# Feed-forward of a decoder trunk: the weight sums of the next column pair are traced amid a pair, the second product starts with another of its seven quarter products, and the residual tiles are loaded back one at a time

## The chip, the cores and the metric

One Trainium2 chip, of which the kernel uses one core (core 0). The time is device microseconds of one whole execution. Before the change three runs took 1507.84, 1508.0 and 1511.98 us; the median is 1508.0 us. The profiled execution took 1507.54 us, of which 1505.8 us are the span that the trace covers.

## The reference

The kernel computes one decoder layer on 1024 rows of width 1024 in float32: three groups of attention heads, an output projection, and a feed-forward part. All that the change touches is the feed-forward part and the final norm:

```python
h2 = rmsnorm(x, norm2_g[l])
u = jnp.square(jax.nn.relu(jnp.einsum('bsd,df->bsf', h2, w_1[l])))   # 1024 -> 4096
x = x + jnp.einsum('bsf,fd->bsd', u, w_2[l])                         # 4096 -> 1024
...
return rmsnorm(x, final_g)
```

## The kernel before

**Precision.** Every float32 factor is split into a high and a low part (hi by ScalarE, lo = value - hi by VectorE), and a product is three matmuls: hi x hi, hi x lo, lo x hi. TensorE is "PE" in the rows, its unit of work here is a matmul of 128x128 weights by 512 columns.

**First product.** The 4096 columns of W1 are worked in 16 pairs of 2 x 128. The first four pairs (NP0) are plain (`hidden`). Pairs 4 to 15 go through `pair_products`: a pair's product is a 2x2 matrix of quarters, and seven quarter products in place of eight are taken, each 12 matmuls (L1339 to L1341), in this order of weights: b11, t2, t3, t1, b21, t4, b22. Here b11, b21, b22 are quarters of the weights themselves; t1 to t4 are sums of quarters, worked out on the chip. On the other side stand quarters of the rows or their sums s1 to s4 (tiles `sr` in the rows), made beforehand.

`pair_weights` makes a pair's weights: two loads of 512 KB (tiles `raw`, L1312, issued by SyncE, "SP"), the split of the first tile (w1h on ScalarE L1327, w1l on VectorE L1328), the four sums (tiles `tr`, VectorE L1324), and their splits (tiles `tw`: hi on ScalarE L1318, lo on VectorE L1319). It is called at the head of `pair_products`, so in the text of the program a pair's weight work stands behind all work of the pair before.

After each quarter product `into` adds it into a half of a hidden tile `ut` (VectorE, L1355), `squared` applies ReLU and square (ScalarE, L1344 and L1345), and at a pair's end five combinations of the four halves (tiles `us`, VectorE L1390) and two halves themselves are written to DRAM, as `u_d[i, j]`; those seven writes are issued by ScalarE (L1391 to L1393).

**Second product.** Seven quarter products again, each over all 16 pairs: `operands(i, spec, j)` loads `u_d[i, j]` (tile `uw`, L1243) and either one quarter of W2 into the same tile (L1246) or two quarters into a tile `w2q` (L1249, L1250), which VectorE adds or subtracts (L1251). Then ScalarE writes the high part (`uwh`, L1254) and VectorE the low (`uwl`, L1255), and 12 matmuls follow (L1399 to L1401). In the table `products` five of seven need two quarters; those at index i = 2 and i = 1 need one. The first four operand sets are requested during the last pair (`ahead`). When a quarter product is finished, it is added into the residual tiles `xa` (L1462), which were stored in DRAM (`xa_d`) and come back by eight loads of 512 KB (L1455), all issued behind the step (n, j) = (0, 4), and behind them in the text nothing else of that step.

**What sets the order.** Each engine runs its instructions in one fixed order. A scheduler (the tile framework) sets it when the kernel is built, from the order of the Python text, the dependences and its own costs; an instruction whose input or buffer is not ready holds up all that stand behind it on that engine. Buffers are pools: `ut`, `tw`, `uw`, `w2q` and `sraw` share ten 4 KB buffers; `raw` has two; `tr` and `us` share eight; `w1h` and `w1l` share four. All PSUM tiles (names pt, psd, s, po in the rows) share eight banks.

Of the kernel before, what the change touches and what calls it, by code (L numbers as in the profile page):

```python
# [19 lines left out]
DM = 1024  # L20
DFF = 4096
NB = 8
# [52 lines left out]
def dap(ap, offset, dims):  # L75
    return bass.AP(tensor=ap.tensor, offset=ap.offset + offset, ap=dims)
# [3 lines left out]
def trunk_kernel(ctx, tc, x, norm1_g, w_in, b_f, lam_q1, lam_k1, lam_q2, lam_k2,  # L80
# [3 lines left out]
    dma = nc.sync.dma_start  # L84
# [28 lines left out]
    def utile(shape, dt, name):  # L113
        return up.tile(shape, dt, tag="u", name=name)
# [7 lines left out]
    def wtile(shape, dt, name):  # L122
        return wp.tile(shape, dt, tag="w", name=name)
# [7 lines left out]
    def ttile(shape, name):  # L131
        return tp.tile(shape, F32, tag="t", name=name)
# [5 lines left out]
    state = {}  # L138
# [40 lines left out]
    def bcast_row(vec, n, name):  # L179
        t = ttile([P, n], name)  # L180
        dma(t, dap(vec, 0, [[0, P], [1, n]]))
        return t
# [1013 lines left out]
    def bank():  # L1196

        p, tag, name = banks[turn[0] % len(banks)]
        turn[0] += 1
        return p.tile([P, 512], F32, tag=tag, name=name)  # L1200
# [3 lines left out]
    NP = DFF // (2 * P)  # L1204
    u_d = dp.tile([7, NP, P, 512], F32, name="u_d")

    def hidden(ws, ut, half):
        (wh, wl), cs = ws, slice(half * 512, (half + 1) * 512)
        ps = bank()
        for k in range(8):  # L1210
            hh = h2[0][half][k // 2][:, k % 2, :]
            hl = h2[1][half][k // 2][:, k % 2, :]
            T.matmul(ps, wh[:, k, :], hh, start=(k == 0), stop=False)
            T.matmul(ps, wh[:, k, :], hl, start=False, stop=False)
            T.matmul(ps, wl[:, k, :], hh, start=False, stop=(k == 7))
        A.activation(ut[:, cs], ps, AF.Relu)
        V.scalar_tensor_tensor(ut[:, cs], ps, 0.0, ut[:, cs], op0=ALU.max, op1=ALU.mult)
# [3 lines left out]
    def w2q(j, right, n):  # L1221
        r0 = (2 * j + right) * P
        return w_2[r0:r0 + P, n * 512:(n + 1) * 512]

    add, sub = ALU.add, ALU.subtract
    products = (
        (0, ((0, 0), (1, 1), add), ((0, 0, add), (1, 1, add))),
        (5, ((0, 1), (1, 1), sub), ((0, 1, add), (1, 1, add))),
        (2, ((1, 1), None, None), ((0, 0, sub), (0, 1, add))),
        (6, ((1, 0), (0, 0), sub), ((0, 0, add), (1, 0, add))),  # L1230
        (4, ((1, 0), (1, 1), add), ((0, 0, add),)),
        (1, ((0, 0), None, None), ((1, 0, add), (1, 1, sub))),
# [5 lines left out]
    def operands(i, spec, j):  # L1238

        alloc = ptile if made[0] % 10 < 2 else htile  # L1240
        made[0] += 1
        raw = utile([P, 2, 512], F32, "uw")
        dma(raw[:, 0, :], u_d[i, j])  # L1243
        q0, q1, op = spec
        if q1 is None:
            dma(raw[:, 1, :], w2q(j, *q0))  # L1246
        else:
            two = utile([P, 2, 512], F32, "w2q")
            dma(two[:, 0, :], w2q(j, *q0))  # L1249
            dma(two[:, 1, :], w2q(j, *q1))  # L1250
            V.tensor_tensor(raw[:, 1, :], two[:, 0, :], two[:, 1, :], op=op)  # L1251
        hi = alloc([P, 2, 512], F32R, "uwh")
        lo = alloc([P, 2, 512], F32R, "uwl")
        A.activation(hi, raw, AF.Copy)  # L1254
        V.tensor_tensor(lo, raw, hi.bitcast(F32), op=ALU.subtract)  # L1255
        return hi, lo
# [3 lines left out]
    NP0 = 4  # L1260
# [48 lines left out]
    def pair_weights(j):  # L1309
        r0, r1 = (rp.tile([P, 8, P], F32, tag="r", name="raw") for _ in range(2))  # L1310
        for r, ft in ((r0, 2 * j), (r1, 2 * j + 1)):
            dma(r, w_1[:, ft * P:(ft + 1) * P].rearrange("(k p) n -> p k n", p=P))  # L1312
        h0, l0 = (wtile([P, 8, P], F32R, n) for n in ("w1h", "w1l"))
        q0, q1 = slice(0, 4), slice(4, 8)
        w = dict(b11=(h0[:, q0], l0[:, q0]), b21=(h0[:, q1], l0[:, q1]))

        def split(name, raw, both):
            A.activation(both[:, 0], raw, AF.Copy)  # L1318
            V.tensor_tensor(both[:, 1], raw, f32(both[:, 0]), op=sub)  # L1319
            w[name] = both[:, 0], both[:, 1]  # L1320

        def weight_sum(name, p0, p1):
            raw = qtile([P, 4, P], F32, "tr")
            V.tensor_tensor(raw, p0, p1, op=sub)  # L1324
            split(name, raw, utile([P, 2, 4, P], F32R, "tw"))
            return raw
        A.activation(h0, r0, AF.Copy)  # L1327
        V.tensor_tensor(l0, r0, f32(h0), op=sub)  # L1328
        t1 = weight_sum("t1", r1[:, q0], r0[:, q0])
        t2 = weight_sum("t2", r1[:, q1], t1)  # L1330
        weight_sum("t3", r1[:, q1], r1[:, q0])
        weight_sum("t4", r0[:, q1], t2)
        split("b22", r1[:, q1], tp.tile([P, 2, 4, P], F32R, tag="t", name="b22"))
        return w
# [8 lines left out]
    def squared(a):  # L1343
        A.activation(a, a, AF.Relu)  # L1344
        A.activation(a, a, AF.Square)  # L1345

    def pair_products(j, ut):

        w = pair_weights(j)
        a11, a21, a12, a22 = ut[0][:, :512], ut[0][:, 512:], ut[1][:, :512], ut[1][:, 512:]  # L1350

        def into(dst, src, a, b):
            ps = bank()
            quarter_product(ps, a, w[b])
            V.tensor_tensor(dst, src, ps, op=add)  # L1355
            return ps
        ps = bank()
        quarter_product(ps, a11q, w["b11"])
        A.activation(a11, ps, AF.Copy)
        into(a12, a11, rows_sum["s2"], "t2")  # L1360
        into(a21, a12, rows_sum["s3"], "t3")
        p5 = into(a22, a21, rows_sum["s1"], "t1")
        V.tensor_tensor(a12, a12, p5, op=add)
        squared(a22)
        for dst, a, b in ((a11, a12q, "b21"), (a21, a22q, "t4"), (a12, rows_sum["s4"], "b22")):
            into(dst, dst, a, b)
            squared(dst)

    ahead = []
    for j in range(NP):  # L1370
        if j == NP - 1:
            ahead += [operands(0, products[0][1], t) for t in range(2)]
        ws, ut = [], []
        for ft in (2 * j, 2 * j + 1):
            if j < NP0:
                ws.append(load_split(w_1[:, ft * P:(ft + 1) * P].rearrange("(k p) n -> p k n", p=P),
                                     [P, 8, P], "w1"))
            ut.append(utile([P, S], F32, "ut"))
        if j < NP0:
            for i, half in ((0, 0), (1, 0), (0, 1), (1, 1)) if j < 2 else ((0, 0), (0, 1), (1, 0), (1, 1)):  # L1380
                hidden(ws[i], ut[i], half)
        else:
            pair_products(j, ut)
        a11, a21, a12, a22 = ut[0][:, :512], ut[0][:, 512:], ut[1][:, :512], ut[1][:, 512:]
        for i, p0, p1, op in ((0, a11, a22, add), (3, a21, a11, sub), (1, a21, a22, add),
                              (2, a11, a12, add), (4, a12, a22, sub)):
            if j == NP - 1 and i == 2:
                ahead += [operands(0, products[0][1], len(ahead) + t) for t in range(2)]
            st = qtile([P, 512], F32, "us")
            V.tensor_tensor(st, p0, p1, op=op)  # L1390
            A.dma_start(u_d[i, j], st)  # L1391
        A.dma_start(u_d[5, j], a11)
        A.dma_start(u_d[6, j], a22)  # L1393
        row_sums(j)
# [49 lines left out]
    for n, (i, spec, dsts) in enumerate(products):  # L1444
        ps = [bank() for _ in range(4)]
        stag = STAG if n == len(products) - 1 else 0
        for j in range(NP - stag):
            ops = ahead.pop(0) if ahead else operands(i, spec, j)
            for m in range(4):
                accumulate(ps[m], m, ops, j == 0, j == NP - 1)  # L1450
            if (n, j) == (0, 4):
                gf_bc = bcast_row(final_g, DM, "gf_bc")
                for sb in range(NB):
                    xa[sb] = vtile([P, DM], F32, "xa") if sb < 6 else ttile([P, DM], "xa")
                    dma(xa[sb], xa_d[sb])  # L1455
        kept = [operands(i, spec, j) for j in range(NP - stag, NP)]
        for m in range(4):
            for j, ops in enumerate(kept):
                accumulate(ps[m], m, ops, False, j == stag - 1)
            for r, c, op in dsts:  # L1460
                x_q = xa[4 * r + m][:, c * 512:(c + 1) * 512]
                V.tensor_tensor(x_q, x_q, ps[m], op=op)  # L1462
            if n == 4:
                finish_row(m)
            elif n == 5:
                begun.append(begin_row(4 + m))
            elif stag:
                end_row(4 + m, begun[m])
# [29 lines left out]
```

## Time and profile before

| what | us |
|---|---|
| median of three runs (lowest, highest) | 1508.0 (1507.84, 1511.98) |
| profiled execution | 1507.54 |
| its span | 1505.8 |
| TensorE (PE) busy | 1428.2, 95% |
| VectorE (DVE) busy | 1008.8, 67% |
| ScalarE (ACT) busy | 728.9, 48% |
| GpSimd (POOL) busy | 175.4, 12% |

The span begins at the first instruction of the trace. The attention part and the first four column pairs fill it up to about 927 us; pairs 4 to 15 run up to 1185.3, the second product up to 1497.5, and the last norm and store up to the end. The number behind a tile name in the order listings is a running number of the build, so a tile of the same pair can have two numbers in the two kernels. "PEclk" is the clock that was granted to TensorE as a share of full speed (2.4 GHz); 0.50 is 1.2 GHz. A row of busy times reads: stretch in us, its length, busy us (and number of instructions) of PE, of its weight loads, of DVE, ACT and POOL, then PEclk, the DMA engines' busy share, and GB/s. In a timeline the bracket at a row's end is how long the engine had been idle and what released it.

### The profile page before, as it was taken

Reading aid. Unit: us, or ns where it says so; the run is one execution under the profiler, and the core shown is the slowest. Engines: PE = TensorE matmul, PEld = TensorE weight load, DVE = VectorE, ACT = ScalarE, POOL = GpSimd, SP = SyncE. Lnnn points to the kernel's source line nnn. Section 1 sums busy time; section 2 is a strip of 40 time slices with the busy share of each in tenths; the row PEclk is TensorE's granted clock in tenths of the full one; section 3 lists DMA queues with packets and bytes.
Section 4 is the critical chain, followed back from the end, with each engine's and each line's share of the span. In section 5 each row is a group of like instructions: output and inputs, shape, how many; then the busy total and the mean of one; then the engine's idle time right before and its main releaser. Section 6 shows DMA issues by size and latency. Waiting matters only on the chain.

```text
span 1505.8 us, 21003 instructions
## 1 busy us (share of the span) xinstructions
PE 1428.2 (95%) x7427; PEld 1185.5 (79%) x7427; DVE 1008.8 (67%) x2090; ACT 728.9 (48%) x1421; POOL 175.4 (12%) x125
## 2 busy tenths in 40 slices
PE   7999999999999989988899998999989899999997
PEld 7988877797878889876687786787768688888886
DVE  5535357757685555577977985577767588786783
ACT  5345456656575555447533423345444335343542
POOL 1021111102022212222301120000000000000000
PEclk8999999999999999999999999999999999999999
DMA  6334455444423121388315243344435899888661
GB/s 219 61 105 115 114 161 148 123 117 118 103 65 98 52 64 38 91 187 259 103 36 161 73 145 133 105 148 153 133 126 180 305 336 366 296 298 270 228 230 56
DMA packets 164265, 230.28 MB, mean 153 GB/s; under 512 B 14942, under 2 KB 89182, under 8 KB 164160
## 3 DMA queue, kind: packets, MB, share of 16 engines
q1 hardware_dynamic: 143232, 194.33, 42.7%
q10 hardware_dynamic: 20928, 34.61, 6.2%
q8 instruction: 58, 0.95, 0.3%
q14 instruction: 47, 0.39, 0.1%
HBM read 170.86 MB, written 56.85 MB: 151 GB/s over the span
## 4 chain that ended last, share of the span: by engine, by line
PE 55%; DVE 6%; ACT 4%; DMA 3%; issue 2%; SPq 0%; ACTq 0%; POOL 0%; DVEq 0%; POOLq 0%
PE pt L1399 3%; PE pt L1400 3%; PE pt L1401 3%; PE po L458 2%; PE psd L296 2%; PE psd L298 2%; PE psd L297 2%; PE pt L438 2%; PE s L1399 2%; PE pt L1339 2%; PE s L1400 2%; PE s L1401 2%; PE pt L1341 2%; PE pt L1340 2%; PE psd L1399 1%
## 5 line engine op out<-in xcount | busy, mean ns | idle before, releaser
L1254 ACT ACTIVATE uwh<-uw 128x1024 fp32r<-128x1024 f32 x112 | 116.2, 1057 | 160.5 <-DVE uw L1251 40.1
L1255 DVE TENSOR_TENSOR uwl<-uw,uwh 128x1024 fp32r<-128x1024 f32 x112 | 134.3, 1222 | 48.1 <-ACT uwh L1254 47.8
L296 PE MATMUL psd<-hT,wqh 128*128 128x512 f32 x384 | 159.2, 414 | 0.4 <-DVE kl L412 0.3
L298 PE MATMUL psd<-hT,wql 128*128 128x512 f32 x384 | 154.1, 401 | 0.9 <-POOL wql L282 0.9
L297 PE MATMUL psd<-hT,wqh 128*128 128x512 f32 x384 | 152.7, 398 | 0.0
L442 DVE TENSOR_TENSOR pTl<-pt,pTh 128x512 fp32r<-128x512 f32 (+1 forms) x160 | 99.6, 631 | 56.1 <-ACT pTh L441 54.7
L326 PE MATMUL psd<-wvh,hT 128*128 128x256 f32 (+1 forms) x384 | 115.1, 301 | 2.9 <-ACT hT L204 1.8
L327 PE MATMUL psd<-wvl,hT 128*128 128x256 f32 (+1 forms) x384 | 110.6, 289 | 2.3 <-POOL wvl L282 2.3
L328 PE MATMUL psd<-wvh,hT 128*128 128x256 f32 (+1 forms) x384 | 110.0, 288 | 0.0
L438 PE MATMUL pt<-ident,prow 128*128 128x128 f32 x572 | 94.5, 278 | 10.6 <-ACT prow L503 7.3
L441 ACT ACTIVATE pTh<-pt 128x512 fp32r<-128x512 f32 (+1 forms) x160 | 86.2, 548 | 37.4 <-PE pt L438 34.5
L282 POOL TENSOR_TENSOR wql<-raw,wqh 128x1024 fp32r<-128x1024 f32 x24 | 58.2, 2428 | 291.6 <-ACT wqh L281 291.6
L438 PEld LDWEIGHTS pt<-ident,prow 128*128 128x128 f32 x572 | 68.9, 142 | 27.4 <-ACT prow L503 11.8
L298 PEld LDWEIGHTS psd<-hT,wql 128*128 128x128 f32 x384 | 72.7, 189 | 15.9 <-POOL wql L282 1.9
L296 PEld LDWEIGHTS psd<-hT,wqh 128*128 128x128 f32 x384 | 73.0, 190 | 11.8 <-DVE kl L412 0.6
L297 PEld LDWEIGHTS psd<-hT,wqh 128*128 128x128 f32 x384 | 72.9, 190 | 10.3
L326 PEld LDWEIGHTS psd<-wvh,hT 128*128 128x128 f32 x384 | 74.4, 194 | 6.3 <-ACT hT L204 3.8
L1390 DVE TENSOR_TENSOR us<-ut 128x512 f32<-128x512 f32 x80 | 54.6, 715 | 34.8 <-ACT ut L1345 34.7
L327 PEld LDWEIGHTS psd<-wvl,hT 128*128 128x128 f32 x384 | 74.7, 194 | 3.9 <-POOL wvl L282 2.9
L458 PE MATMUL po<-pTh,vt 128*128 128x128 f32 (+1 forms) x284 | 73.7, 280 | 4.2 <-ACT pTh L441 3.1
L328 PEld LDWEIGHTS psd<-wvh,hT 128*128 128x128 f32 x384 | 74.3, 194 | 1.5 <-issue 0.8
L458 PE MATMUL po<-pTl,vt 128*128 128x128 f32 (+1 forms) x284 | 71.4, 293 | 3.5 <-DVE pTl L442 3.0
(381 smaller groups left out, 3823.6 us busy)
## 6 DMA issues: line engine op xcount, KB each, us to landing
w2q<-in_w_dram SPq DMA_DIRECT2D x160, 256.0 KB
uw<-u_d SPq DMA_DIRECT2D x112, 256.0 KB
u_d<-us ACTq DMA_DIRECT2D x80, 256.0 KB
raw<-in_w_in_dram SPq DMA_DIRECT2D x34, 512.0 KB
raw<-in_w_dram SPq DMA_DIRECT2D x32, 512.0 KB
sa<-aqk_d SPq DMA_DIRECT2D x32, 256.0 KB
u_d<-ut ACTq DMA_DIRECT2D x32, 256.0 KB
uw<-in_w_dram SPq DMA_DIRECT2D x32, 256.0 KB
```

The source lines that it names most:

```text
L296: T.matmul(ps, wh[:, k, :], hh, start=(k == 0), stop=False)
L297: T.matmul(ps, wh[:, k, :], hl, start=False, stop=False)
L298: T.matmul(ps, wl[:, k, :], hh, start=False, stop=(k == 7))
L326: T.matmul(dst, hh, wh[:, k % 4, :], start=(k == 0), stop=False)
L327: T.matmul(dst, hh, wl[:, k % 4, :], start=False, stop=False)
L328: T.matmul(dst, hl, wh[:, k % 4, :], start=False, stop=(k == 7))
L438: T.transpose(pt[:, i * P:(i + 1) * P], b, ident)
L442: V.tensor_tensor(lo[:, :n], pt[:, :n], hi[:, :n].bitcast(F32), op=ALU.subtract)
L458: T.matmul(po[:, cols:cols + n], lhs, pT[part][:, c0:c0 + n], start=(first and part == 0), stop=(last and part == 1))
L1254: A.activation(hi, raw, AF.Copy)
L1255: V.tensor_tensor(lo, raw, hi.bitcast(F32), op=ALU.subtract)
L1399: T.matmul(ps, hi[:, 0, ms], hi[:, 1, :], start=first, stop=False)
```

## The change

Three edits, none of which adds or removes an instruction; on each engine there are as many after as before.

1. `pair_weights(j + 1)` is called in the middle of pair j, behind the fourth quarter product and its `squared`, and for pair 4 behind the last plain pair. The weights are handed over in `state["w"]`.
2. In `products` the rows stand in the order i = 2, 5, 0, 6, 4, 1, 3 in place of 0, 5, 2, 6, 4, 1, 3: the second product begins with one of the two that need a single quarter of W2 (two loads of 256 KB for a step, no sum on VectorE). `ahead` names its index accordingly.
3. The residual tiles are requested one at a time, behind every second step of the first of these seven, each placed in SyncE's order behind the latest `uw` load (`tc.issue_after`); the load of the final norm's gains (L181 in `bcast_row`) moves to (n, j) = (1, 0).

```diff
@@ -1224,9 +1224,9 @@
 
     add, sub = ALU.add, ALU.subtract
     products = (
+        (2, ((1, 1), None, None), ((0, 0, sub), (0, 1, add))),
+        (5, ((0, 1), (1, 1), sub), ((0, 1, add), (1, 1, add))),
         (0, ((0, 0), (1, 1), add), ((0, 0, add), (1, 1, add))),
-        (5, ((0, 1), (1, 1), sub), ((0, 1, add), (1, 1, add))),
-        (2, ((1, 1), None, None), ((0, 0, sub), (0, 1, add))),
         (6, ((1, 0), (0, 0), sub), ((0, 0, add), (1, 0, add))),
         (4, ((1, 0), (1, 1), add), ((0, 0, add),)),
         (1, ((0, 0), None, None), ((1, 0, add), (1, 1, sub))),
@@ -1240,7 +1240,7 @@
         alloc = ptile if made[0] % 10 < 2 else htile
         made[0] += 1
         raw = utile([P, 2, 512], F32, "uw")
-        dma(raw[:, 0, :], u_d[i, j])
+        state["uw"] = dma(raw[:, 0, :], u_d[i, j]).ins
         q0, q1, op = spec
         if q1 is None:
             dma(raw[:, 1, :], w2q(j, *q0))
@@ -1346,7 +1346,7 @@
 
     def pair_products(j, ut):
 
-        w = pair_weights(j)
+        w = state["w"]
         a11, a21, a12, a22 = ut[0][:, :512], ut[0][:, 512:], ut[1][:, :512], ut[1][:, 512:]
 
         def into(dst, src, a, b):
@@ -1362,6 +1362,8 @@
         p5 = into(a22, a21, rows_sum["s1"], "t1")
         V.tensor_tensor(a12, a12, p5, op=add)
         squared(a22)
+        if j + 1 < NP:
+            state["w"] = pair_weights(j + 1)
         for dst, a, b in ((a11, a12q, "b21"), (a21, a22q, "t4"), (a12, rows_sum["s4"], "b22")):
             into(dst, dst, a, b)
             squared(dst)
@@ -1369,7 +1371,7 @@
     ahead = []
     for j in range(NP):
         if j == NP - 1:
-            ahead += [operands(0, products[0][1], t) for t in range(2)]
+            ahead += [operands(products[0][0], products[0][1], t) for t in range(2)]
         ws, ut = [], []
         for ft in (2 * j, 2 * j + 1):
             if j < NP0:
@@ -1379,13 +1381,15 @@
         if j < NP0:
             for i, half in ((0, 0), (1, 0), (0, 1), (1, 1)) if j < 2 else ((0, 0), (0, 1), (1, 0), (1, 1)):
                 hidden(ws[i], ut[i], half)
+            if j == NP0 - 1:
+                state["w"] = pair_weights(NP0)
         else:
             pair_products(j, ut)
         a11, a21, a12, a22 = ut[0][:, :512], ut[0][:, 512:], ut[1][:, :512], ut[1][:, 512:]
         for i, p0, p1, op in ((0, a11, a22, add), (3, a21, a11, sub), (1, a21, a22, add),
                               (2, a11, a12, add), (4, a12, a22, sub)):
             if j == NP - 1 and i == 2:
-                ahead += [operands(0, products[0][1], len(ahead) + t) for t in range(2)]
+                ahead += [operands(products[0][0], products[0][1], len(ahead) + t) for t in range(2)]
             st = qtile([P, 512], F32, "us")
             V.tensor_tensor(st, p0, p1, op=op)
             A.dma_start(u_d[i, j], st)
@@ -1448,11 +1452,13 @@
             ops = ahead.pop(0) if ahead else operands(i, spec, j)
             for m in range(4):
                 accumulate(ps[m], m, ops, j == 0, j == NP - 1)
-            if (n, j) == (0, 4):
-                gf_bc = bcast_row(final_g, DM, "gf_bc")
-                for sb in range(NB):
+            if n == 0 and j % 2 == 0:
+                sb = j // 2
+                with tc.issue_after(state["uw"]):
                     xa[sb] = vtile([P, DM], F32, "xa") if sb < 6 else ttile([P, DM], "xa")
                     dma(xa[sb], xa_d[sb])
+            if (n, j) == (1, 0):
+                gf_bc = bcast_row(final_g, DM, "gf_bc")
         kept = [operands(i, spec, j) for j in range(NP - stag, NP)]
         for m in range(4):
             for j, ops in enumerate(kept):
```

The first listing is VectorE's order before the change, at the end of pair 9 and the start of pair 10. `ut_10571` and `us_...` belong to pair 9; `tr_10737` to `tw_10754` are pair 10's weight sums and their low parts, and `ut_10728<-ut_10727,psd_10774` takes up pair 10's second quarter product (the one with t2).

```order
L1355 TENSOR_TENSOR ut_10571<-ut_10571,s_10694 128x512
L1390 TENSOR_TENSOR us_10716<-ut_10570,ut_10571 128x512
L1390 TENSOR_TENSOR us_10719<-ut_10570,ut_10571 128x512
L1390 TENSOR_TENSOR us_10722<-ut_10571 128x512
L1324 TENSOR_TENSOR tr_10737<-raw_10730,raw_10729 128x512
L1324 TENSOR_TENSOR tr_10742<-raw_10730,tr_10737 128x512
L1324 TENSOR_TENSOR tr_10747<-raw_10730 128x512
L1319 TENSOR_TENSOR tw_10739<-tr_10737,tw_10739 128x512
...
L1319 TENSOR_TENSOR tw_10754<-tr_10752,tw_10754 128x512
L1355 TENSOR_TENSOR ut_10728<-ut_10727,psd_10774 128x512
```

The same place after the change: the `tr` and `tw` tiles that follow pair 9's last `us` are those of pair 11 (10827 and up). Those of pair 10 stand one pair earlier, behind pair 8's last `us`.

```order
L1394 TENSOR_TENSOR us_10750<-ut_10601,ut_10602 128x512
L1394 TENSOR_TENSOR us_10753<-ut_10602 128x512
L1324 TENSOR_TENSOR tr_10827<-raw_10820,raw_10819 128x512
L1324 TENSOR_TENSOR tr_10832<-raw_10820,tr_10827 128x512
L1355 TENSOR_TENSOR ut_10759<-ut_10758,psd_10774 128x512
L1319 TENSOR_TENSOR tw_10829<-tr_10827,tw_10829 128x512
L1319 TENSOR_TENSOR tw_10834<-tr_10832,tw_10834 128x512
L1324 TENSOR_TENSOR tr_10837<-raw_10820 128x512
L1355 TENSOR_TENSOR ut_10758<-ut_10759,s_10788 128x512
L1324 TENSOR_TENSOR tr_10842<-raw_10819,tr_10832 128x512
L1319 TENSOR_TENSOR tw_10839<-tr_10837,tw_10839 128x512
```

So pair 10's sums no longer stand between pair 9's last combination and the quarter product of pair 10 that needs them; the sums found there have a whole pair until they are due.

TensorE's order before at the start of pair 10: `pt_10760` is its first quarter product (with w1h and w1l), `pt_10802` the fourth (tw_10739, which is t1), `pt_10819` the fifth (b21, a half of w1h), and `psd_10774` the second (tw_10744, which is t2).

```order
L1339 MATMUL pt_10760<-h2001_8821,w1h_10733 128x512
L1340 MATMUL pt_10760<-h2101_8825,w1h_10733 128x512
L1341 MATMUL pt_10760<-h2001_8821,w1l_10734 128x512
L1339 MATMUL pt_10802<-sr_9461,tw_10739 128x512
L1340 MATMUL pt_10802<-sr_9463,tw_10739 128x512
L1339 MATMUL pt_10819<-h2002_8822,w1h_10733 128x512
L1339 MATMUL psd_10774<-sr_9630,tw_10744 128x512
L1340 MATMUL psd_10774<-sr_9632,tw_10744 128x512
```

And after the change, the same place:

```order
L1339 MATMUL pt_10760<-h2001_8821,w1h_10666 128x512
L1340 MATMUL pt_10760<-h2101_8825,w1h_10666 128x512
L1341 MATMUL pt_10760<-h2001_8821,w1l_10667 128x512
L1339 MATMUL psd_10774<-sr_9630,tw_10677 128x512
L1340 MATMUL psd_10774<-sr_9632,tw_10677 128x512
L1341 MATMUL psd_10774<-sr_9630,tw_10677 128x512
L1339 MATMUL psd_10774<-sr_9630,tw_10677 128x512
L1340 MATMUL psd_10774<-sr_9632,tw_10677 128x512
```

Before, single matmuls of three quarter products stand mixed behind the first one; after, the twelve of the second product follow the twelve of the first without anything between.

SyncE's order before, at the start of the second product; `xa` are the residual tiles, of which one has been requested earlier and seven stand here in a row ahead of the next operand set (`uw_11801`, the sixth of its product, whose two w2q loads follow).

```order
L1455 DMA xa_11787<-xa_d_8751 128x1024
L1455 DMA xa_11789<-xa_d_8751 128x1024
L1455 DMA xa_11791<-xa_d_8751 128x1024
L1455 DMA xa_11793<-xa_d_8751 128x1024
L1455 DMA xa_11795<-xa_d_8751 128x1024
L1455 DMA xa_11797<-xa_d_8751 128x1024
L1455 DMA xa_11799<-xa_d_8751 128x1024
L1243 DMA uw_11801<-u_d_9168 128x512
```

After, the stretch that begins with the fourth operand set (each now has two loads, both into `uw`):

```order
L1243 DMA uw_11682<-u_d_9168 128x512
L1246 DMA uw_11682<-in_w_2_dram 128x512
L1459 DMA xa_11713<-xa_d_8751 128x1024
L1459 DMA xa_11739<-xa_d_8751 128x1024
L1243 DMA uw_11753<-u_d_9168 128x512
L1246 DMA uw_11753<-in_w_2_dram 128x512
L1459 DMA xa_11772<-xa_d_8751 128x1024
L1243 DMA uw_11774<-u_d_9168 128x512
```

The residual loads now stand singly or in twos between operand sets.

## Rows read from the trace of the kernel before

**Rows 1.** Busy time by stage, in the columns told above.

```profile
927.10:1185.30 258.20, 242.69 (x1013) 191.89 (x1012) 179.52 (x270) 115.33 (x179) 0.00 (x0) 0.97 0.44 150
1185.30:1208.50 23.20, 17.22 (x67) 13.79 (x66) 10.69 (x14) 6.14 (x8) 0.00 (x0) 0.85 1.01 374
1208.50:1497.50 289.00, 288.99 (x1275) 238.91 (x1273) 211.05 (x284) 120.99 (x143) 0.00 (x0) 1.00 0.76 260
```

**Rows 2.** Same view, every stretch with half clock between 927 and 1210.

```profile
935.35:938.76 3.41, 3.20 (x8) 2.53 (x9) 1.36 (x3) 0.59 (x2) 0.00 (x0) 0.50 0.96 284
959.24:962.65 3.41, 3.41 (x10) 2.56 (x9) 2.56 (x5) 1.24 (x3) 0.00 (x0) 0.50 0.58 168
1102.60:1109.43 6.83, 6.22 (x14) 4.44 (x15) 4.53 (x7) 3.22 (x5) 0.00 (x0) 0.50 0.53 156
1201.59:1208.41 6.82, 4.26 (x10) 3.40 (x11) 3.81 (x5) 2.11 (x2) 0.00 (x0) 0.50 1.02 368
```

**Rows 3.** TensorE's waits from 927 to 1210: total us, times, longest.

```profile
PE pt L1339 <- ACT tw L1318: 6.7, 3, 2.4
PE psd L1339 <- ACT tw L1318: 6.1, 2, 3.1
PE s L1399 <- ACT uwh L1254: 6.0, 1, 6.0
PE s L1341 <- DVE tw L1319: 1.6, 2, 1.0
```

**Rows 4.** Timeline of TensorE at the start of pair 10: start, duration, what, idle.

```profile
1054.14 0.40 PE L1339 MATMUL pt<-h,w1h 128*128 128x512 f32 x1
...
1056.72 0.40 PE L1341 MATMUL pt<-h,w1l 128*128 128x512 f32 x1
1059.47 0.50 PE L1339 MATMUL pt<-sr,tw 128*128 128x512 f32 x1 [2.35 <-ACT tw L1318]
```

**Rows 5.** Timeline of VectorE at the same place.

```profile
1055.10 0.69 DVE L1390 TENSOR_TENSOR us<-ut 128x512 f32<-128x512 f32 x1
1056.86 1.29 DVE L1390 TENSOR_TENSOR us<-ut 128x512 f32<-128x512 f32 x2 [1.07 <-ACT ut L1345]
1058.07 0.68 DVE L1324 TENSOR_TENSOR tr<-raw 128x512 f32<-128x512 f32 x1
```

**Rows 6.** Timeline of ScalarE at the same place.

```profile
1055.82 0.33 ACTq L1391 DMA_DIRECT2D u_d<-us  x1
1056.19 0.63 ACT L1345 ACTIVATE ut<-ut 128x512 f32<-128x512 f32 x1 [0.34 <-ACT ut L1344]
...
1058.79 1.96 ACT L1318 ACTIVATE tw<-tr 128x512 fp32r<-128x512 f32 x3 [1.96 <-DVE tr L1324]
```

**Rows 7.** Costs by line on VectorE, pairs 4 to 15: busy us, mean ns, idle before.

```profile
L1319 DVE TENSOR_TENSOR tw<-tr,tw 128x512 fp32r<-128x512 f32 x48 | 30.7, 686 | 6.3 <-ACT tw L1318 6.3
...
L1328 DVE TENSOR_TENSOR w1l<-raw,w1h 128x1024 fp32r<-128x1024 f32 x11 | 13.5, 1223 | 7.0 <-ACT w1h L1327 7.0
```

**Rows 8.** A load of `raw`: SyncE's issue, then ScalarE's first use.

```profile
1082.17 2.74 SPq L1312 DMA_DIRECT2D raw<-in_w_dram  x2
```

**Rows 9.** ScalarE's first use of the tile just loaded.

```profile
1086.22 1.06 ACT L1327 ACTIVATE w1h<-raw 128x1024 fp32r<-128x1024 f32 x1 [0.56 <-DMA raw<-in_w_dram]
```

**Rows 10.** Timeline of SyncE at the start of the second product.

```profile
1185.85 6.66 SPq L1455 DMA_DIRECT2D xa<-xa_d  x7
```

**Rows 11.** Chain of waits that ended last in 1184 to 1206: start, duration, what.

```profile
1189.09 8.69 DMA u_d<-us
...
1197.79 4.45 DMA w2q<-in_w_dram
...
1202.26 0.70 DVE uw L1251
```

**Rows 12.** Costs by line on VectorE from 1208 to 1500.

```profile
L1255 DVE TENSOR_TENSOR uwl<-uw,uwh 128x1024 fp32r<-128x1024 f32 x106 | 126.9, 1222 | 45.3 <-ACT uwh L1254 45.0 <-DMA w2q<-in_w_dram 0.2
```

**Rows 13.** Busy time in a stretch of products with two quarters each.

```profile
1316.00:1400.00 84.00, 84.00 (x372) 69.58 (x371) 60.62 (x69) 33.20 (x34) 0.00 (x0) 1.00 0.82 277
```

## The prediction, on record before the result

> **What bounds the kernel now.** I read the page's busy shares first, then busy time cut at the stage borders, then TensorE's list of waits, then the timelines of three engines around one such wait, and last the chain of waits at the start of the second product. TensorE is the bound nearly everywhere: from 1208.5 to the end of the second product it is busy 288.99 of 289.00 us, while in pairs 4 to 15 it is busy 242.69 of 258.20 us, and 17.22 of the 23.20 us between [rows 1]. So only those last two stretches have something to give, besides the few microseconds behind 1497.5, which the change does not touch.
>
> The same rows give the pace. 289.00 us over 1275 matmuls is 0.2267 us for one; with w1 weights eleven steps take 1056.72 - 1054.14 = 2.58 us, 0.2345 each [rows 1, 4]. The twelve pairs have 12 x 84 = 1008 matmuls, of which 24 per pair (b11, b21) have w1 weights: 720 x 0.2267 + 288 x 0.2345 = 163.2 + 67.5 = 230.7 us. In the first stretch a few of the second product's matmuls are run too, early (some four, 0.9 us). 258.2 - 0.9 - 230.7 leaves **26.6 us lost in the pairs**. I can name 20.8 of them: 6.7 + 6.1 + 1.6 = 14.4 us of waits for `tw` [rows 3], and the half clock behind such waits: 3.20 + 3.41 + 6.22 = 12.83 us of matmuls at 0.50, that is at 1.2 GHz, half of which, 6.4 us, would not have been spent at 2.4 GHz [rows 2]. The other 5.8 us I take to be starts held up in small pieces, where single matmuls of several products stand mixed.
>
> What ends these waits stands in three timelines of one place. TensorE ends its first product's last matmul about 1057 and starts on `tw` at 1059.47, having waited 2.35 us for ScalarE [rows 4]. ScalarE had been idle 1.96 us for VectorE's `tr` [rows 6]. VectorE begins `tr` at 1058.07, directly behind two `us` that it could only begin at 1056.86, since they wait for ScalarE's square of the last quarter [rows 5]. The `tr` sum itself reads nothing but `raw`. It is late only by its place in VectorE's order.
>
> At the start of the second product the chain is another: an `u_d` write takes 8.69 us to land, the `w2q` load behind it 4.45, then VectorE's sum 0.70 (and ScalarE's split), until TensorE starts, 5.98 us idle [rows 11, 3]. In that time SyncE has issued seven residual tiles in 6.66 us [rows 10], and the DMA engines are full: share 1.01, 374 GB/s [rows 1].
>
> **Part 1, the earlier weight sums.** Nothing is added: 4 `tr`, 4 `tw` and the rest stay. In the new order each pair's `tr` and `tw` stand a whole pair (84 matmuls, 230.7 / 12 = 19.2 us) ahead of their use, and TensorE's twelve matmuls of t2 stand whole behind those of b11. The wait for `tw` goes. What could be late next?
> - VectorE: 21 operations of 0.687 and one of 1.22 make 15.7 us of a pair's 19.2 [rows 7]. The `us` of the last quarter end, as in the row now, about 4 us into the pair (1058.15 - 1054.14) [rows 4, 5]; two `tr` follow, and the uptake of the second product, due at 5.5 us (24 matmuls), is about on time. Being late there would only hold a PSUM bank, of which there are eight.
> - ScalarE: 115.33 us over twelve pairs, 9.6 each [rows 1], plus seven issues of 0.33 [rows 6], 11.9 of 19.2 us.
> - Raw loads: two buffers; a load into them can be issued once the fourth `tr` has read the last one; it stands behind the uptake of the third product (8.25 us into a pair), so about 9.6, and landing takes 1086.22 - 1082.17 = 4.05 us [rows 8, 9]. At 13.7 it can be split, and TensorE needs the split at 19.2.
> - Buffers: two `ut`, four `tw` in use and four `tw` of the next pair fill the ten. The next pair's third and fourth `tw` thus wait for the `ut` of the pair before, that is for its `u_d` writes, some 3 us before the pair's start, to land. Wanted at 7 to 8 us, this leaves some 10 us, against a longest landing of 8.69 in the fullest stretch [rows 11].
>
> So I take all 26.6 us as gained. The bounds: 0 us, should the order only trade one wait for another, and 28.8, should the w1 matmuls too run at 0.2267 (288 x 0.0078 = 2.2 more). The named part alone is 20.8.
>
> The Trainium skill ("Perfetto Trace Analysis", Optimization Strategy) has a rule that speaks against this: a gap that repeats on the engine that should be busy can mean that there is not enough buffer space for the next tile. By that, an earlier place in the order would give nothing. Here the waits end with VectorE's own queue and not with a release of a buffer [rows 5, 6], so I give it little; with ten buffers exactly filled afterwards it keeps a chance below.
>
> **Parts 2 and 3, the start of the second product.** The first operand sets need two loads and no sum in place of three and a sum, and one of the ten buffers in place of two; and the seven tiles no longer stand ahead of them. The gain is at most the 5.98 us of waiting and half of the 4.26 us at half clock [rows 3, 2]: 5.98 + 2.13 = 8.1. (Check: 23.20 - 67 x 0.2267 = 8.0.) The first seventh then moves 16 x 512 KB and the eight residual tiles of 512 KB, 12.6 MB in 16 x 12 x 0.2267 = 43.5 us: 289 GB/s, against 374 already seen [rows 1]. I take 8.1. The lower bound is below nothing: afterwards four products of two quarters stand in a row, 768 KB in 2.72 us, 289 GB/s, where before they were broken by a light one. A stretch of such products shows 277 GB/s at a share of 0.82 with TensorE busy 84.00 of 84.00 us [rows 13], so this costs nothing until the memory gives less than it does there. If it gave the 260 GB/s of the whole stage [rows 1], each of four products would take 43.5 x 289/260 = 48.4 us, 19.5 us lost in all; VectorE's share, 16 x (1.22 + 0.69) = 30.6 us of 43.5 besides the residual adds [rows 12, 7], is no limit.
>
> A second place for the Trainium skill ("TensorE: Matmul & The Clock Gate", Terms): it puts the penalty of a slow clock at the time spent at it times (1 - K/N). The four half-clock stretches are 3.41 + 3.41 + 6.83 + 6.82 = 20.47 us [rows 2], which would make 10.2 us. I count 6.4 + 2.1 = 8.5 from the matmuls alone, since TensorE idled in part of these stretches and I have that under the waits.
>
> **The sum.** 26.6 + 8.1 = 34.7 us. The span goes from 1505.8 to 1471.1, the profiled execution from 1507.54 to 1472.8; the median before stands 0.46 above that execution, so 1473.3, and I predict **1473.5**. Its own range is 1470.5 to 1479: from the faster w1 matmuls (2.2) to the unnamed 5.8 staying.
>
> **The rivals.**
> - A: the start of the second product still waits. For it: the last pair's writes took 8.69 us to land, and they are still written there. Against it: that was with seven residual tiles issued among them. All of 8.1 us stays: 1473.3 + 8.1 = 1481.4.
> - B: half of the pairs' loss stays, for in-order queues: VectorE is at 15.7 of 19.2 us, and `tr` of the pair after next now stand directly ahead of an uptake. 13.3 us stays: 1486.6.
> - C, slower: the full buffer pool. If `u_d` writes land late, ScalarE waits in its order at the third `tw`, with ReLU and square of the running pair queued behind, and VectorE's combinations and TensorE's next products wait for those. It begins to cost at about 10 us for a landing, but ScalarE has 19.2 - 11.9 = 7.3 us to catch up, so TensorE loses what a landing takes beyond 17.3 us. Slower than before from 17.3 + 34.7/12 = 20.2 us on; at 20.6 it would be 1473.3 + 12 x 3.3 = 1512.9. Against it: such landings are twice the worst row, and the pairs have a DMA share of 0.44 [rows 1].
> - D: the pairs gain nothing, since the wait is one of buffers (or the scheduler's order hides no other wait); only the start of the second product does: 1508.0 - 8.1 = 1499.9. If the four heavy products then starve as bounded above, this would be no change or slower.
>
> **Chances.** Forecast 0.66, A 0.13, B 0.11, C 0.05, D 0.05. What a measurement of this kernel tells from no change is about 0.3%, 4.5 us. C is slower; D splits into 0.02 faster and 0.03 no change. Faster 0.92, same 0.03, slower 0.05. The range of 8 in 10 takes the forecast's own range and A, and reaches over B for what the bounds leave unknown: 1470 to 1487.
>
> **What would show it.** TensorE's list of waits without the two `tw` rows of 6 us and without `uwh`; no half-clock stretch between pair 4 and the second product; about 231 us for twelve pairs; residual loads spread over the first seventh. If TensorE instead waits for ScalarE's `ut` or its own banks, with ScalarE waiting for `u_d` writes, C was right; if a row of `uwh` waiting for `w2q` appears in the four heavy products, my reading of the DMA's room was wrong.

## The result, and the profile after

Four runs of the changed kernel took 1469.95 to 1474.18 us, median 1472.78; the kernel before, with one more run beside them, has a median of 1508.74. The ratio is 0.9756, 95% interval 0.9733 to 0.9778. The forecast was 1473.5 within 1470 to 1487. The profiled execution took 1474.18 us, with a span of 1472.5. TensorE, VectorE, ScalarE and the DMA requests count as many instructions in the trace as before; only its semaphore instructions are 80 more.

Busy time by stage of the kernel after, in the columns of [rows 1]: the twelve pairs, the first seventh of the second product (one of its seven quarter products), the second product as a whole, and a stretch of heavy quarter products (those that need two quarters of W2; the other two are called light) as in [rows 13].

```profile
928.63:1159.33 230.70, 230.70 (x1009) 189.36 (x1008) 176.27 (x261) 116.43 (x179) 0.00 (x0) 1.00 0.48 165
1159.33:1202.84 43.51, 43.51 (x193) 36.05 (x192) 28.05 (x30) 18.90 (x19) 0.00 (x0) 1.00 1.01 370
1159.33:1464.20 304.87, 304.81 (x1345) 252.15 (x1343) 222.49 (x300) 125.69 (x148) 0.00 (x0) 1.00 0.78 274
1282.00:1366.00 84.00, 84.00 (x372) 69.60 (x371) 61.89 (x72) 32.78 (x31) 0.00 (x0) 1.00 0.84 294
```

TensorE is busy for every one of the 230.70 us of the pairs, at the full clock. Before, the stretch from the first matmul of pair 4 to the last one of the second product was 1497.48 - 927.12 = 570.36 us long; now it is 1464.13 - 928.63 = 535.50 us, 34.86 us less. The list of TensorE's waits, whose four rows stand in [rows 3] for before, has no row at all from 928 to 1464, and none of the half-clock stretches of [rows 2] is left.

The place of [rows 4 to 6], the start of pair 10, on TensorE after the change; start, duration, what:

```profile
1043.98 0.40 PE L1339 MATMUL pt<-h,w1h 128*128 128x512 f32 x1
...
1046.56 0.39 PE L1341 MATMUL pt<-h,w1l 128*128 128x512 f32 x1
1046.79 0.39 PE L1339 MATMUL psd<-sr,tw 128*128 128x512 f32 x1
```

And on VectorE:

```profile
1046.54 1.30 DVE L1394 TENSOR_TENSOR us<-ut 128x512 f32<-128x512 f32 x2 [0.47 <-ACT ut L1345]
1047.75 0.68 DVE L1324 TENSOR_TENSOR tr<-raw 128x512 f32<-128x512 f32 x1
1048.47 0.69 DVE L1324 TENSOR_TENSOR tr<-raw,tr 128x512 f32<-128x512 f32 x1
1049.78 0.69 DVE L1355 TENSOR_TENSOR ut<-ut,psd 128x512 f32<-128x512 f32 x1 [0.61 <-PE psd L1341]
```

The `us` still wait for the last square, and a `tr` still follows them: 3.77 us behind the start of the pair (1047.75 - 1043.98), where it was 3.93 (1058.07 - 1054.14). So VectorE has become hardly earlier in that place. But the `tr` there is another pair's, and TensorE finds its `tw` ready at 1046.79. Ahead of the uptake at 1049.78 VectorE even stands idle for 0.61 us, so the two sums make nobody wait.

SyncE, where the second product's first sets are requested:

```profile
1144.29 0.41 SPq L1243 DMA_DIRECT2D uw<-u_d  x1
1144.76 0.50 SPq L1246 DMA_DIRECT2D uw<-in_w_dram  x1
1147.19 1.69 SPq L1459 DMA_DIRECT2D xa<-xa_d  x2
1148.97 0.38 SPq L1243 DMA_DIRECT2D uw<-u_d  x1
1149.41 0.42 SPq L1246 DMA_DIRECT2D uw<-in_w_dram  x1
```

In place of seven residual tiles in a row from 1185.85, directly at the start of the second product [rows 10], two go out 12 us ahead of it, and operand sets follow at once.

### The profile page after: what moved, and what is told of

Same layout as the page of the kernel before. It is cut to its first block, busy times and chain, and to the rows that moved or that the text cites. A ratio compares the mean times of both kernels' runs of the same rounds, so it can differ in the third digit from the quotient of the medians.

```text
span 1472.5 us, 21083 instructions
## 1 busy us (share of the span) xinstructions
PE 1415.8 (96%) x7427; PEld 1183.3 (80%) x7427; DVE 1008.6 (68%) x2090; ACT 729.5 (50%) x1421; POOL 175.2 (12%) x125
## 4 chain that ended last, share of the span: by engine, by line
PE 59%; DVE 4%; ACT 3%; DMA 2%; issue 2%; SPq 0%; ACTq 0%; POOL 0%; DVEq 0%; POOLq 0%
PE pt L1403 3%; PE pt L1404 3%; PE pt L1405 3%; PE po L458 2%; PE psd L296 2%; PE pt L1340 2%; PE pt L1341 2%; PE pt L1339 2%; PE psd L297 2%; PE psd L298 2%; PE s L1403 2%; PE s L1404 2%; PE s L1405 2%; PE pt L438 2%; PE psd L1403 1%
## 5 line engine op out<-in xcount | busy, mean ns | idle before, releaser
L451 ACT ACTIVATE u<-po 64x256 f32<-64x256 f32 x96 | 36.5, 380 | 75.0 <-PE po L458 70.9
```

## The experiments

**Each edit by itself, and in pairs.** The diffs are parts of the one above, with "..." where lines are left out. Each ratio is against runs of the kernel before that were taken beside the run; their medians lie between 1508.65 and 1510.54 us. All times of pairs and of the second product are from the first matmul to the first (or last) of the next stage, in one profiled execution.

Edit 1 alone:

```diff
-        w = pair_weights(j)
+        w = state["w"]
...
+        if j + 1 < NP:
+            state["w"] = pair_weights(j + 1)
...
+            if j == NP0 - 1:
+                state["w"] = pair_weights(NP0)
```

Expected: 

> Edit 1 alone (the next pair's weight sums traced amid a pair; products table and residual loads as before). Theory (TensorE waited for the weight sums only because of their place in VectorE's order): the twelve pairs take 230.7 us instead of about 257, no wait of TensorE for tw; the gap in the second product stays near 6 us plus half clock, so 1508 - 26.6 = about 1481. Rival D (the wait is one of buffers): pairs stay at about 257, time 1508. Rival B: pairs about 244, time about 1495.

Measured: 1478.58 us (4 runs; ratio 0.9782, interval 0.9757 to 0.9807).

```profile
927.32:1158.02 230.70, 230.70 (x1009) 189.37 (x1008) 177.82 (x265) 115.81 (x178) 0.00 (x0) 1.00 0.49 167
1158.02:1469.06 311.04, 307.98 (x1345) 254.04 (x1343) 220.66 (x296) 126.23 (x149) 0.00 (x0) 0.99 0.77 267
```

The pairs are at 230.70 us, so the first edit alone does all that was done there. The gap in the second product is there, but shorter: 3.1 us of waiting in place of 6.0 [rows 3]. Its chain is the one of [rows 11] with smaller members:

```profile
1162.83 7.76 DMA u_d<-us
...
1170.66 3.05 DMA w2q<-in_w_dram
...
1173.73 1.06 ACT uwh L1254
```

A write to DRAM lands and gives its buffer back, then the load into that buffer follows. Together they take 10.8 us where they took 13.1. The expectation had this gap at about 6 us, as before. The half clock behind it has remained, so the second product is only some 2.0 us shorter than before (311.0 us; before 312.2, and 0.9 more of it that ran early, amid the last pair).

Edit 2 alone:

```diff
-        (0, ((0, 0), (1, 1), add), ((0, 0, add), (1, 1, add))),
+        (2, ((1, 1), None, None), ((0, 0, sub), (0, 1, add))),
...
```

Expected: 

> Edit 2 alone (second product begins with the product that needs one quarter of W2; weight sums and residual loads as before). Pairs stay at about 257 us. Theory: the sixth operand set, behind the seven residual tiles in SyncE's order, no longer waits for a w2q buffer, that is for the 8.69 us of a u_d write, but still for the seven issues and its own load: a gap of about 2 us instead of 6, no half clock, 1508 - 6 = about 1502. If this edit alone closes the gap, 1500; if the gap is the residual tiles' doing, it stays and the time is 1508.

Measured: 1504.01 us (8 runs; ratio 0.995, interval 0.9933 to 0.9968). Waits of TensorE from 927 to 1500:

```profile
PE pt L1339 <- ACT tw L1318: 6.7, 3, 2.3
PE psd L1339 <- ACT tw L1318: 6.1, 2, 3.1
PE s L1341 <- DVE tw L1319: 1.5, 2, 1.0
PE s L1399 <- ACT uwh L1254: 1.4, 1, 1.4
PE s L1339 <- ACT tw L1318: 0.2, 1, 0.2
```

The waits for `tw` are those of before. The wait for `uwh` has fallen from 6.0 to 1.4 us, no half clock is behind it, and the second product takes 306.0 us in place of 312.2. What is left of it, in the chain of waits from 1185 to 1203:

```profile
1187.38 5.66 DMA u_d<-us
...
1193.06 0.32 SPq L1455
...
1193.93 6.28 DMA uw<-in_w_dram
```

A residual tile's issue (L1455) waits for a landing write, the next operand set stands behind it in SyncE's order, and its load then takes 6.28 us among the residual tiles.

Edit 3 alone:

```diff
-            if (n, j) == (0, 4):
...
-                for sb in range(NB):
+            if n == 0 and j % 2 == 0:
+                sb = j // 2
+                with tc.issue_after(state["uw"]):
...
```

Expected: 

> Edit 3 alone (residual tiles one by one; heavy product first, weight sums as before). Pairs stay at about 257 us. If the gap is the residual tiles' doing: no wait for uwh in the second product, 1500. If it is the buffers' and the heavy sets': the w2q load still waits for a landing write, gap 2 to 6 us, 1502 to 1508; and 16 sets of 768 KB plus eight tiles of 512 KB, 16.8 MB in 43.5 us, would need 386 GB/s, above the 374 seen, so up to 2 us more could be lost in that seventh.

Measured: 1508.86 us (10 runs; ratio 0.9993, interval 0.9973 to 1.0013). Nothing is won. The gap at the sixth operand set is gone, but one at the end of the first seventh has come, when VectorE's residual adds stand ahead of the next operands; TensorE's wait there, and the seventh's busy times:

```profile
PE psd L1400 <- DVE uwl L1255: 3.8, 1, 3.8
```

```profile
1185.40:1228.90 43.50, 43.31 (x184) 33.62 (x183) 27.31 (x32) 15.11 (x17) 0.00 (x0) 1.00 1.03 380
```

By the estimate in the expectation the heavy sets and the residual tiles together ask for 386 GB/s, and the DMA engines, at a share of 1.03, give 380. The operands have no lead left when the adds come: ScalarE's splits wait for loads to land, as here at the end of the seventh.

```profile
1225.80 1.06 ACT L1254 ACTIVATE uwh<-uw 128x1024 fp32r<-128x1024 f32 x1 [2.03 <-DMA w2q<-in_w_dram]
```

Edits 1 and 2, without 3 (the diff is against the changed kernel):

```diff
...
+            if (n, j) == (0, 4):
+                gf_bc = bcast_row(final_g, DM, "gf_bc")
+                for sb in range(NB):
...
```

Expected: 

> Edits 1 and 2 without 3 (all residual tiles requested in a row as before). Theory: pairs 230.7 us; a gap of at most about 2 us where the seven residual tiles stand ahead of the sixth operand set: 1473 to 1476. If edit 3 is what closes the gap: it stays at 6 to 8 us, about 1481.

Measured: 1475.3 us (4 runs; ratio 0.9756, interval 0.9725 to 0.9786). One short wait of TensorE is left, 0.4 us for `uwl`; the second product takes 305.58 us. The third edit is thus worth 0.8 us on top of the other two (305.58 - 304.80), which the times cannot tell.

Edits 1 and 3, without 2 (the first line of the table as before).

Expected: 

> Edits 1 and 3 without 2 (heavy product first). Theory (a heavy first seventh with the residual tiles beside it asks for more than the DMA gives): pairs 230.7 us, no wait at the sixth operand set, but a wait at the end of the first seventh, as with edit 3 alone (3.9 us there) where VectorE's eight residual adds stand ahead of the next operands' low part; 1475 to 1478. Rival (it is the order of the loads alone that counts): no wait at all, 1472.8 as with all three edits.

Measured: 1479.84 us (4 runs; ratio 0.9803, interval 0.9771 to 0.9834). Pairs 230.70 us; one wait of 3.8 us at the end of the first seventh, as with edit 3 alone. The chain there, with the last five of VectorE's eight residual adds (L1468 in this kernel) ahead of the sum of the next set:

```profile
1205.65 3.07 DVE xa L1468 x5
1208.72 0.61 DVE uw L1251
...
1209.50 1.07 ACT uwh L1254
...
1210.61 0.80 PE psd L1403
```

At the end of the wait a stretch at half clock begins:

```profile
1209.20:1216.03 6.83, 5.42 (x13) 4.26 (x14) 6.20 (x9) 4.22 (x5) 0.00 (x0) 0.50 0.74 231
```

Half of its 5.42 us of matmuls, 2.7 us, is lost besides the wait. The expectation, 1475 to 1478 us, had the wait but no half clock behind it, and was missed by 1.8 us. The second product takes 313.1 us; with edit 1 alone it took 311.0. So spreading the loads pays nothing with a heavy product first.

Edits 2 and 3, without 1 (`pair_weights(j)` at the head of `pair_products` as before).

Expected: 

> Edits 2 and 3 without 1 (weight sums as before). Theory (the effects of the edits lie in different stretches and add up): pairs stay at 257 to 259 us with the waits for tw of before (about 15 us and the half clock behind them), no wait in the second product, 304.8 us: 1508 - 7.4 = about 1500.5. If the changed start of the second product also helped the last pairs, it would be lower, towards 1495.

Measured: 1499.31 us (5 runs; ratio 0.9941, interval 0.992 to 0.9963). Pairs 257.3 us, with the waits for `tw` of before, and no wait in the second product, which takes 303.9 us (a few of its matmuls run early, amid the last pair, as they did before). From the first matmul of pair 4 to the last one of the second product it is 561.2 us here, 9.1 less than before; 541.7 with edit 1 alone, 28.6 less; 535.5 with all, 34.9 less. 9.1 and 28.6 are together 2.9 too many. Some 2.0 of them are what edit 1 alone already takes off the second product, which counts twice in this sum; the other 0.9 lies in the pairs, which are that much shorter here than in the kernel before (257.3 and 258.2), and its cause stays open.

**Is the repeated wait one of buffers?** The kernel before and the changed kernel, both with eight buffers in place of ten:

```diff
-    up = pool("up", 10)
+    up = pool("up", 8)
```

Before, expected: 

> The kernel before with 8 in place of 10 buffers in that pool. Theory (its waits for tw came from VectorE's order): pairs still about 258 us; only the start of the second product can get longer, by some us. Rival D (the repeated gap is one of buffers): with two fewer the waits for tw grow, by 2 us or more per pair, pairs 280 us or more, 1530 or more.

Measured: 1523.3 us (5 runs; ratio 1.008, interval 1.0051 to 1.0109). Waits of TensorE from 926 on:

```profile
PE pt L1339 <- ACT tw L1318: 6.7, 3, 2.3
PE psd L1339 <- ACT tw L1318: 6.1, 2, 3.1
PE s L1399 <- ACT uwh L1254: 5.3, 1, 5.3
PE s L1341 <- DVE tw L1319: 1.5, 2, 1.0
PE psd L1341 <- DVE tw L1319: 0.4, 1, 0.4
PE s L1339 <- ACT tw L1318: 0.2, 1, 0.2
```

With two buffers fewer the waits for `tw` are those of [rows 3] to within 0.1 us. Pairs and second product take 260.3 and 312.2 us. The pairs' 2.1 us more are not waiting: TensorE is busy 245.07 us there in place of 242.69, at a granted clock of 0.96 in place of 0.97. Of the 16.2 us between the two profiled executions (1523.71 and 1507.54) 13.8 are spent ahead of the pairs, which now begin at 940.90 (before 927.12). Ten buffers are wanted there, by earlier stages.

After, expected: 

> The changed kernel with 8 in place of 10 buffers in the pool of ut, tw, uw and w2q. Theory (a place early in the order, with slack of some 10 us against a landing write): two buffers less are paid out of the slack, the pairs stay within 1 us of 230.7; in the second product four heavy sets ahead instead of five, at most a few us: 1473 to 1478. Rival C (the ten exactly filled buffers are what the pairs live from): the next pair's sums wait for the previous pair's writes, ScalarE with them, 2 us or more per pair, pairs 255 us or more, 1497 or more.

Measured: 1487.01 us (4 runs; ratio to the kernel before with its ten buffers 0.9844, interval 0.9804 to 0.9884). The expectation for the whole time was missed for the same reason, a start of the pairs at 943.12; pairs and second product are untouched:

```profile
943.12:1173.82 230.70, 230.70 (x1009) 189.32 (x1008) 176.29 (x261) 115.98 (x179) 0.00 (x0) 1.00 0.48 165
1173.82:1478.62 304.80, 304.80 (x1345) 252.06 (x1343) 223.31 (x299) 125.39 (x148) 0.00 (x0) 1.00 0.80 274
```

ScalarE does wait for writes to land now (a row of its list of waits from 928 to 1160; with ten buffers the list has no such row), and the lead of a whole pair covers it:

```profile
ACT tw L1318 <- DMA u_d<-us: 3.5, 2, 1.8
```

**How far ahead must the sums stand?** The call behind the pair's last product:

```diff
-        if j + 1 < NP:
-            state["w"] = pair_weights(j + 1)
         for dst, a, b in (...):
             into(dst, dst, a, b)
             squared(dst)
+        if j + 1 < NP:
+            state["w"] = pair_weights(j + 1)
```

Expected: 

> The changed kernel, but the next pair's weight sums are traced at the end of the pair's products, just ahead of the five combinations, and not in the middle. Theory (what counts is to stand ahead of the combinations that wait for the last squares): pairs 230.7 us, 1472.8 as the changed kernel. Rival (half a pair of lead is what counts): waits for tw come back, pairs 240 us or more, 1482 or more.

Measured: 1470.93 us (2 runs; ratio 0.9743, interval 0.9713 to 0.9773); pairs 230.70 us, second product 304.80, no wait. Through the twelve pairs TensorE, ScalarE and VectorE run their instructions in the same order as in the changed kernel: the scheduler has put the sums in the same places. So the text only has to stand ahead of the five combinations; "amid the pair" is not what counts. Since the order is the same, how much lead the sums need was not measured. That it is nearly 2 us lower is no gain: its pairs begin at 926.86, the changed kernel's at 928.63, and from there on both take 535.50 us.

**Two tries at the pace of the w1 matmuls**, 0.2345 us each where all others in the two stages take 0.2267.

```diff
...
-        A.activation(h0, r0, AF.Copy)
-        V.tensor_tensor(l0, r0, f32(h0), op=sub)
+        split("b11", r0[:, q0], wtile([P, 2, 4, P], F32R, "w1h"))
+        split("b21", r0[:, q1], wtile([P, 2, 4, P], F32R, "w1l"))
```

Expected: 

> The changed kernel with the high and low parts of b11 and b21 each kept together in one tile like tw (four splits in place of two, same buffers of the same pool). It asks why matmuls with w1 weights take 0.2345 us each and all others 0.2267. If it is how the weights lie in a tile: pairs 228.5 us, 2.2 less. If it is the pool's place in memory or something else: pairs 230.7, time unchanged at 1472.8.

Measured: 1474.02 us (4 runs; ratio 0.9761, interval 0.9728 to 0.9793). Pairs 229.78 us, 0.9 less, too little to show in the times. First and last of the twelve matmuls with b11 (now named w1h), then with b21 (w1l):

```profile
949.71 0.40 PE L1338 MATMUL po<-h,w1h 128*128 128x512 f32 x1
...
952.28 0.40 PE L1340 MATMUL po<-h,w1h 128*128 128x512 f32 x1
...
960.70 0.39 PE L1338 MATMUL psd<-h,w1l 128*128 128x512 f32 x1
...
963.19 0.39 PE L1340 MATMUL psd<-h,w1l 128*128 128x512 f32 x1
```

Eleven steps take 2.57 us with b11 and 2.49 with b21: 0.234 and 0.226. One of the two has gone to the pace of the others, the other has not.

```diff
+    wp = pool("wp", 4)
     hp = pool("hp", 16)
...
-    wp = pool("wp", 4)
```

Expected: 

> The changed kernel with the pool of w1h and w1l made before the pool of the h tiles, so that both lie at other addresses. It asks again for the 0.2345 us of matmuls with w1 weights; with high and low part in one tile b21 went to 0.2267 and b11 stayed at 0.233. If the addresses of the tiles make the difference, the pace of some or all w1 matmuls changes, pairs 228.5 to 230.7 us; if not, 230.7 and no change of the pace.

Measured: 1474.45 us (2 runs; ratio 0.9767, interval 0.9738 to 0.9795), pairs 230.70 us. The place of the pool changes nothing.

## Why the prediction was right, point by point

- **The pairs' loss of 26.6 us, all gained.** Right in size: 230.7 us forecast from the pace and the count of matmuls, 230.70 measured. The 5.8 us that had no name went too, so they hung on the same order; edit 1 alone takes them along. The trace of the kernel before names most of them. TensorE's list of waits from 927 to 1210 has two rows more than [rows 3], 0.9 us:

```profile
PE s L1339 <- ACT tw L1318: 0.5, 2, 0.2
PE psd L1341 <- DVE tw L1319: 0.4, 1, 0.4
```

And at full clock, these waits taken out, 37 steps from one matmul to the next are longer than their pace by 0.03 to 0.29 us, 4.6 us in all, nearly all with `tw` weights; after the change there is no such step. That fits what I had taken them for.

- **The cause, VectorE's order.** Shown: with eight buffers in that pool the waits are the same, and with the sums ahead of the combinations, and no buffer more, they are gone. Rival D falls with that, and B with the 230.70. The rule of the Trainium skill on gaps that repeat ("Perfetto Trace Analysis", Optimization Strategy) gives missing buffers as a possible cause; the measurement here speaks against it, 6.7 and 6.1 us of waiting with ten buffers as with eight.
- **The buffers exactly filled.** This step failed, on the careful side. I counted two `ut`, two of the pair before and eight `tw` against ten buffers, as if all lived at once. With ten buffers ScalarE's list has no wait for a `u_d` write in the pairs, so they don't. Even with eight it has only two, of 1.8 us at most, and TensorE has none. Rival C rested on that count; no run had TensorE lose anything to it, so its price for long landings was not tested.
- **The start of the second product, 8.1 us.** Right as a sum for edits 2 and 3 together: the second product went from 313.1 us (312.2, and the 0.9 that ran early) to 304.8, 8.3 less; with the pairs' 26.6 that makes the 34.86 us measured, against 34.7. No wait for `uwh` is left, so A falls. I gave the two edits one term and did not say which closes the gap; A was priced as all or nothing. The runs show that the light product does most (a wait of 6.0 us falls to 1.4, to 0.4 with edit 1 as well), and that the spread loads pay only with it: by themselves they move the gap to the seventh's end.
- **The DMA's room.** I had 289 GB/s for the first seventh, as if loads came evenly. They run ahead of TensorE, at 370 GB/s and a share of 1.01. The conclusion stood, TensorE is busy 43.51 of 43.51 us. The worry about four heavy products in a row was void, 84.00 of 84.00 at 294 GB/s.
- **The sum.** Of the 34.86 us won, 33.36 show between the two profiled executions (1507.54 - 1474.18), since the pairs of the second began 1.51 us later (928.63, not 927.12), in the part ahead of what the change touches. In the profiles of the kernels with ten buffers that start lies between 926.44 and 930.61; that is about as wide as the spread of single runs of the changed kernel (1469.95 to 1474.18).

## What to carry to other kernels

When the engine that bounds the time waits, follow the releaser one step further than the list of waits goes: to what stood directly ahead of it in its own engine's order. Work that reads only early data must not stand, in the text, behind work that waits for the last result of a stage; here it was enough to move it just ahead of that. Of loads that collide at the start of a stage, make the stage begin with its lightest step before spreading the loads: in this kernel spread loads beside heavy steps only moved the wait.

## What was not expected

Matmuls of the same shape and type run at two paces, 0.2267 and 0.2345 us, and the slower goes with the tiles w1h and w1l. With the halves of a part kept in one tile, b21 came to 0.226 and b11 stayed at 0.234; another place of the pool did nothing. Twelve pairs at one pace would be 228.5 us, 2.2 less. What makes the difference stays open.
